# Turning the HGRN2 gate product on VectorE, with its moves pinned in the queue

## The chip, the cores and the metric

The program runs on 1 core of a Trainium2 chip. The metric is the device time of one execution in microseconds (us). Before the change the median of three runs is 398.56 us (398.11 to 400.23).

## The reference, cut to what matters

Two layers of a decoder trunk over 256 tokens of width 1024. In each layer one projection of the normalised input gives ten column groups of 512; three branches turn them into outputs, which are gated, joined and projected back:

```python
q_a, k_a, v_a, q_h, f_h, i_h, q_m, z = jnp.split(proj, split_points, axis=-1)
qa = partial_rope(rms_norm(q_a ..., moba_q_norm[l]), positions)
ka = partial_rope(rms_norm(k_a ..., moba_k_norm[l]), positions)
o_a = moba_attention(qa, ka, va).reshape(B, S, G)          # 8 heads of 64, causal
o_h = hgrn2_chunkwise(q_h, f_h, i_h, lb_all[l] ...)        # 4 heads of 128, gated recurrence
o_h = rms_norm(o_h, hgrn_o_norm[l]).astype(x.dtype).reshape(B, S, G)
o_m = memory_attention(qm, km, vm).reshape(B, S, G)        # 4 heads of 128, 256 memory tokens
y = jnp.concatenate([o_a, o_h, o_m], axis=-1) * jax.nn.silu(z)
x = x + y @ w_out[l]
```

All is f32. The part at issue is the middle third of `y`: `o_h` normalised per head, times its gain `hgrn_o_norm`, times `silu(z_h)`. The kernel calls it `zh`.

## The kernel before, in words

Every large product is made to f32 precision from two rounded parts: a weight tile of 128x1024 arrives by DMA as `wr`, ScalarE (ACT) casts it to the high part `wh` (L173, or L176 when a gain per row is multiplied in), VectorE (DVE) subtracts for the low part `wl` (L185 or L188), and TensorE (PE) runs three passes. `slot` keeps up to five loads, three `wh` and two `wl` ahead of PE. There are four `wr` buffers, three of `wh` and three of `wl`; a cast therefore waits until PE has read the tile three places earlier for the last time.

Each layer takes 60 such tiles in a fixed order: 8 of the memory's keys and values (first), forget logits, HGRN2 queries, MoBA keys, HGRN2 inputs, MoBA queries, `zh`, memory queries, MoBA values (4 tiles each), the gates of MoBA (A0 to A3 below) and of the memory branch (M0 to M3), and 12 tiles of `w_out`, those that multiply `zh` first (`KT_ORDER`).

The branches run as generators beside this stream: `step` moves each of them on by one `yield` at every half tile. That gives the program order, and so the priorities; the order in which each engine issues its instructions is then set by a scheduler that times the whole program by its own model. Instructions given to `keep_in_program_order` are not moved against each other; the weight loads go through `load`, which does that.

`zh` must stand with its columns on the partitions before `w_out` can use it. `y_transpose` (L733 to L747) does that: for each half of the tokens four PE transposes of 128x128 into a tile `sd` of PSUM (one of four side tiles), then ACT writes the high part with the gain (L740) and DVE the low part (L741). The keys of memory and MoBA and the MoBA probabilities `P` go another way, through `across` (L88 to L107): DVE turns blocks of 32x32 into `blk` (L94), a DMA writes `blk` to DRAM as `there` (L100), and four DMAs read it back with the blocks in place (L105). All of these are issued by the queue of SP, in between the weight loads. There is one `blk` buffer and there are two `there`.

The rotary tables `rtA` and `rtB` (L533 to L537) are made once by POOL, for both layers and for query and key; `g_qk` multiplies the projected keys or queries by them (`kr`, L896).

## Time and profile before

| | |
|---|---|
| median of the runs | 398.56 us (398.11 to 400.23) |
| the profiled execution, its own time | 399.08 us |
| its span | 397.3 us |
| PE, busy | 391.6 us (99%), 2887 matmuls |
| PE weight loads, busy | 326.9 us (82%) |
| DVE, busy | 312.2 us (79%) |
| ACT, busy | 258.4 us (65%) |
| POOL, busy | 53.0 us (13%) |
| DMA | 78.25 MB, mean 197 GB/s |

How to read it: times inside the trace count from the start of the span. PE's busy time covers matmuls that overlap in the array, so a pause shorter than a matmul's own length is not seen in it; the distance from one start to the next shows it. The granted clock of PE is full in every slice of the page. A row of the timeline gives the start, the length, engine, line, operation, tiles and count; for engines other than PE the start of the next row says how long an instruction held its engine, since neighbours overlap by about a tenth of a microsecond.

### The profile page before, as it was taken

What the parts mean: (1) busy time and instruction counts of PE and PEld (TensorE: products, weight loads), DVE (VectorE), ACT (ScalarE), POOL (GpSimd) and SP (SyncE); (2) the same over time, 40 slices, a digit from 0 to 9 for tenths busy, and PEclk for the clock granted to TensorE, in tenths of its full rate; (3) what the DMA queues carried; (4) which work ended last, traced back from release to release, by engine and by line L of the source; (5) the groups of instructions that cost most, each with busy time, mean ns of one, the idle gap of its engine ahead of it and who ended that gap; (6) DMA issues with size and microseconds to landing.
All of it is one profiled execution on the core that took longest, in us unless ns stands there. A gap on an engine that the chain in (4) does not pass through costs nothing.

```text
span 397.3 us, 7614 instructions
## 1 busy us (share of the span) xinstructions
PE 391.6 (99%) x2887; PEld 326.9 (82%) x2887; DVE 312.2 (79%) x604; ACT 258.4 (65%) x428; POOL 53.0 (13%) x79
## 2 busy tenths in 40 slices
PE   8999999999999999999999999999999999999996
PEld 6888888778788888878888888888888888888785
DVE  4789979898559997965577689899856799795643
ACT  5998756556768879554375776455855895982540
POOL 2013400704101200000000040031150030000000
PEclk9999999999999999999999999999999999999999
DMA  8976775368535997327554558544854188943522
GB/s 273 412 294 221 237 220 162 110 214 265 170 104 189 247 281 228 111 87 255 185 204 168 177 195 283 196 153 165 260 174 153 54 273 254 283 144 108 184 80 107
DMA packets 25509, 78.25 MB, mean 197 GB/s; under 512 B 3072, under 2 KB 7552, under 8 KB 25472
## 3 DMA queue, kind: packets, MB, share of 16 engines
q1 hardware_dynamic: 25184, 77.61, 59.3%
q8 instruction: 23, 0.38, 0.4%
q10 hardware_dynamic: 288, 0.15, 0.1%
q14 instruction: 14, 0.11, 0.1%
HBM read 71.46 MB, written 6.29 MB: 196 GB/s over the span
## 4 chain that ended last, share of the span: by engine, by line
PE 86%; DVE 6%; DMA 3%; POOL 2%; issue 1%; ACT 1%; SPq 0%; DVEq 0%; ACTq 0%
PE acc L227 58%; PE acc L1149 15%; PE sd L227 6%; PE sd L231 3%; DVE wl L185 2%; DMA kn<-there 1%; POOL rka L893 1%; PE sd L1112 1%; PE sd L440 1%; DMA gT<-in_gains_dram 1%; DMA there<-blk 1%; DVE blk L94 1%; ACT wh L173 1%; PE sd L737 0%; PE sd L1056 0%
## 5 line engine op out<-in xcount | busy, mean ns | idle before, releaser
L185 DVE TENSOR_TENSOR wl<-wr,wh 128x1024 fp32r<-128x1024 f32 x104 | 126.3, 1218 | 41.2 <-ACT wh L173 41.2
L173 ACT CAST wh<-wr 128x1024 fp32r<-128x1024 f32 x104 | 108.9, 1051 | 67.9 <-PE acc L227 37.2
L227 PE MATMUL acc<-wh,hT 128*128 128x512 f32 x384 | 124.8, 396 | 0.0
L227 PEld LDWEIGHTS acc<-wh,hT 128*128 128x128 f32 x384 | 71.8, 188 | 16.0 <-issue 0.7
L227 PE MATMUL acc<-wl,hT 128*128 128x512 f32 x192 | 75.2, 392 | 0.6 <-DVE wl L185 0.6
L227 PE MATMUL acc<-hT,wh 128*128 128x512 f32 x256 | 66.0, 395 | 0.0
L227 PEld LDWEIGHTS acc<-hT,wh 128*128 128x128 f32 x256 | 45.7, 189 | 8.6 <-ACT kn L595 0.4
L227 PEld LDWEIGHTS acc<-wl,hT 128*128 128x128 f32 x192 | 36.1, 188 | 7.8 <-DVE wl L185 0.9
L1149 PE MATMUL acc<-wl,yh 128*128 128x512 f32 (+1 forms) x96 | 37.4, 390 | 0.1
L227 PEld LDWEIGHTS acc<-hT,wl 128*128 128x128 f32 x256 | 35.1, 190 | 2.6
L1149 PE MATMUL acc<-wh,yl 128*128 128x512 f32 (+1 forms) x96 | 37.2, 388 | 0.0
L227 PE MATMUL acc<-hT,wl 128*128 128x256 f32 x256 | 36.4, 282 | 0.0
L1149 PE MATMUL acc<-wh,yh 128*128 128x512 f32 (+1 forms) x96 | 29.8, 388 | 0.0
L176 ACT ACTIVATE wh<-wr,gT 128x1024 fp32r<-128x1024 f32 (+1 forms) x21 | 19.4, 945 | 9.8 <-PE acc L227 4.0
L227 PE MATMUL acc<-wh,mTh 128*128 128x512 f32 x64 | 25.5, 401 | 0.2 <-DVE mTh L379 0.2
L188 DVE SCALAR_TENSOR_TENSOR wl<-wr,gT,wh 128x1024 fp32r<-128x1024 f32 (+1 forms) x21 | 21.0, 1027 | 5.7 <-ACT wh L176 5.7
L227 PE MATMUL acc<-wh,mTl 128*128 128x512 f32 x64 | 24.8, 390 | 0.0
L979 ACT ACTIVATE P<-P,nba,rq 128x128 f32<-128x128 f32 (+1 forms) x32 | 17.1, 537 | 8.1 <-DVE nba L973 8.1
L1149 PEld LDWEIGHTS acc<-wl,yh 128*128 128x128 f32 x96 | 18.0, 188 | 4.4 <-DVE wl L185 1.0
L1149 PEld LDWEIGHTS acc<-wh,yh 128*128 128x128 f32 x96 | 17.9, 188 | 3.9 <-ACT wh L173 0.4
L1149 PEld LDWEIGHTS acc<-wh,yl 128*128 128x128 f32 x96 | 18.0, 188 | 3.6
L227 PE MATMUL acc<-wl,mTh 128*128 128x512 f32 x64 | 20.2, 392 | 0.0
(220 smaller groups left out, 569.0 us busy)
## 6 DMA issues: line engine op xcount, KB each, us to landing
wr<-in_w_in_dram SPq DMA_DIRECT2D x80, 512.0 KB, 4.3
wr<-in_w_out_dram SPq DMA_DIRECT2D x24, 512.0 KB, 4.3
wr<-in_w_mem_kv_dram SPq DMA_DIRECT2D x15, 512.0 KB, 4.9
there<-blk SPq DMA_DIRECT2D x4, 768.0 KB, 3.7
PT<-there SPq DMA_DIRECT2D x16, 192.0 KB, 6.0
there<-blk SPq DMA_DIRECT2D x4, 512.0 KB, 3.2
xs<-in_x_dram SPq DMA_DIRECT2D x2, 512.0 KB, 8.4
memr<-in_mem_dram SPq DMA_DIRECT2D x2, 512.0 KB, 6.7
```

What stands on the lines that cost most here:

```text
L94: nc.vector.transpose(blk.rearrange("p c (n i) -> p c n i", n=n), src.rearrange("p (n c i) -> p c n i", n=n, c=4))
L173: nc.scalar.copy(whs[i], raws[i])
L176: nc.scalar.activation(whs[i][:, sl], raws[i][:, sl], AF.Copy, scale=gT[:, g:g + 1])
L185: nc.vector.tensor_tensor(wls[i], raws[i], whs[i].bitcast(F32), op=OP.subtract)
L188: ins = nc.vector.scalar_tensor_tensor(wls[i][:, sl], in0=raws[i][:, sl], scalar=gT[:, g:g + 1], in1=whs[i][:, sl].bitcast(F32), op0=OP.mu ...
L227: nc.tensor.matmul(o, lhsT=a, rhs=b, start=s, stop=e)
L231: tc.keep_in_program_order(nc.tensor.matmul(o, lhsT=a, rhs=b, start=True, stop=True))
L440: ins = nc.tensor.transpose(pt[:, j * 256 + t * 128:j * 256 + (t + 1) * 128], xn[t][:, k * 128:(k + 1) * 128], ident)
L893: nc.gpsimd.tensor_tensor(r[:, t8], ms[:, t8], pw[:, :8], op=OP.pow)
L979: nc.scalar.activation(P[:, i, kc[t]], P[:, i, kc[t]], AF.Exp, bias=nb[:, c:c + 1], scale=rq[:, r:r + 1], accum_out=sm[:, c:c + 1])
L1112: nc.tensor.transpose(pt[:, i * 256 + t * 128:i * 256 + (t + 1) * 128], P[:, t, i, b * 128:(b + 1) * 128], ident)
L1149: ins = nc.tensor.matmul(a, lhsT=y, rhs=wt[:, cs], start=n == (0 if to is None else nk - 2) and j == 0, stop=n == nk - 1 and j == 2)
```

## The change

Four things. `y_turned` takes the place of `y_transpose`: `zh` goes through `across` as the keys do, with the turned blocks staged in the buffer of the HGRN2 query (`hq0`, free by then), comes back into `zh` itself, and is split by `unstripped` (two casts on ACT, two subtractions on DVE). The gain `hgrn_o_norm` is multiplied into the four `w_out` tiles of that branch instead of into `zh`. The moves in `across` are issued with `load`, so the scheduler no longer moves them against each other or against the weight loads. The setup loses two of its `yield`s, makes the key's rotary tables before the query's, and gives control back only after layer 0.

```diff
-        nc.sync.dma_start(there.rearrange("q j c r -> (q j) c r"), blk)
+        load(there.rearrange("q j c r -> (q j) c r"), blk)
...
-            nc.sync.dma_start(dst[c * 32:c * 32 + 32], there[:, :, c].rearrange("q j r -> j q r"))
+            load(dst[c * 32:c * 32 + 32], there[:, :, c].rearrange("q j r -> j q r"))
...
+    def strip_of(o, t):
+        return o[:, :, t * 128:(t + 1) * 128].rearrange("p h (q i) -> p h q i", q=4)
+
+    def unstripped(oh, ol, a):
+        for t in range(2):
+            src, to = strips(a)[:, :, t], strip_of(oh, t)
+            nc.scalar.copy(to, src)
+            nc.vector.tensor_tensor(strip_of(ol, t), src, to.bitcast(F32), op=OP.subtract)
...
-            chunks.append(("O", dram(w_out, (l * DMIX + kt * 128) * D, [[D, 128], [1, D]]), None))
+            chunks.append(("O", dram(w_out, (l * DMIX + kt * 128) * D, [[D, 128], [1, D]]),
+                           GR_O + l if kt // 4 == H_ else None))
...
         periods(2, 0, 0.0)
         take(2, 0, 0, 1)
-        yield
         take(1, 11, 2, 3)
         take(2, 0, 2)
         take(0, 22, 3)
-        yield
...
-            for q in range(2):
+            for q in (1, 0):
...
-            yield
+                if l == 0:
+                    yield
...
-    def y_transpose(l, t, gain):
...
+    def y_turned(l):
+        flat = zh.rearrange("p t s -> p (t s)")
+        yield from turned(flat, "hq0")
+        unstripped(*y_tiles(H_), flat)
+        yield
+        for k in range(4):
+            done.add(f"y{4 * H_ + k}_{l}")
...
-        yield 2
-        for t in range(2):
-            yield from y_transpose(l, t, gT[:, GR_O + l:GR_O + l + 1])
+        yield from y_turned(l)
```

What it does to the order is seen on three engines. First ACT, layer 0, before: the casts of the gate tiles M1 (`wh_1865`), M2 (`wh_1903`) and M3 (`wh_1932`), and the exponentials of the two memory units (`P_1713` and `P_1781`).

```order
L173 CAST wh_1865<-wr_1773 128x1024
L310 COPY al_1910<-acc_1874 128x256
L712 ACT_TABLE_LOAD
L712 ACTIVATE sg_1888<-as_1825 128x512
L1094 ACT_TABLE_LOAD
L1094 ACTIVATE P_1713,smm0_1749<-sd_1714,nbm0_1748,qmr_1603 128x256 x2
L1094 ACTIVATE P_1713,smm0_1749<-sd_1715,nbm0_1748,qmr_1603 128x256 x2
L173 CAST wh_1903<-wr_1826 128x1024
L310 COPY al_1936<-acc_1913 128x256
L1094 ACTIVATE P_1781,smm1_1810<-sd_1782,nbm1_1809,qmr_1603 128x256 x2
L1094 ACTIVATE P_1781,smm1_1810<-sd_1783,nbm1_1809,qmr_1603 128x256 x2
L173 CAST wh_1932<-wr_1863 128x1024
```

The same place now; M1 is `wh_1857`, M2 `wh_1895`, the units are `P_1708` and `P_1769`.

```order
L183 CAST wh_1857<-wr_1761 128x1024
L320 COPY al_1902<-acc_1866 128x256
L721 ACT_TABLE_LOAD
L721 ACTIVATE sg_1880<-as_1815 128x512
L1092 ACT_TABLE_LOAD
L1092 ACTIVATE P_1708,smm0_1737<-sd_1709,nbm0_1736,qmr_1603 128x256 x2
L1092 ACTIVATE P_1708,smm0_1737<-sd_1710,nbm0_1736,qmr_1603 128x256 x2
L320 COPY al_1934<-acc_1905 128x256
L1092 ACTIVATE P_1769,smm1_1800<-sd_1770,nbm1_1799,qmr_1603 128x256 x2
L1092 ACTIVATE P_1769,smm1_1800<-sd_1771,nbm1_1799,qmr_1603 128x256 x2
L183 CAST wh_1895<-wr_1816 128x1024
L122 CAST yh1_1912<-zh_169 128x4x128 x2
```

The cast of M2 stood between the two units' exponentials and stands behind both now; the two casts of the turned `zh` follow it.

PE at the same place, before: the matmuls of M0 (`wh_1828`, `wl_1867`), of M1 (`wh_1865`, `wl_1905`) and the start of the first MoBA output product (`PT` by `va`, 8 matmuls in all, of which one row is shown).

```order
L227 MATMUL acc_1939<-hT_160,wh_1828 128x512 x8
L227 MATMUL acc_1939<-hT_160,wl_1867 128x256 x8
L227 MATMUL acc_1969<-hT_160,wh_1865 128x512 x6
L227 MATMUL sd_1976<-PT_1701,va_1796 64x256
```

PE now, from A2's second part (`wl_1765`) to the same product: A3 is `wh_1763`, M0 `wh_1818`, M1 `wh_1857`, M2 `wh_1895`.

```order
L237 MATMUL acc_1866<-hT_160,wl_1765 128x256 x8
L237 MATMUL acc_1905<-hT_160,wh_1763 128x512 x8
L237 MATMUL acc_1905<-hT_160,wl_1820 128x256 x8
L237 MATMUL acc_1937<-hT_160,wh_1818 128x512 x8
L237 MATMUL acc_1937<-hT_160,wl_1859 128x256 x8
L237 MATMUL acc_1967<-hT_160,wh_1857 128x512 x8
L237 MATMUL acc_1967<-hT_160,wl_1897 128x256 x8
L237 MATMUL acc_2033<-hT_160,wh_1895 128x512 x8
L237 MATMUL sd_1974<-PT_1696,va_1784 64x256
```

The MoBA product stood inside M1 and stands behind the first eight matmuls of M2 now; the memory scores that stood inside A3 (two groups of six) stand ahead of A2.

DVE in layer 0 where the keys meet their tables (`kr`), before:

```order
L766 TENSOR_TENSOR hQb_793<-hQ_712,hT4_1056 128x64x8
L767 TENSOR_TENSOR hK_565<-hKb_794,hT4_1056 128x64x8
L783 COPY_PREDICATED hSd_162<-mk_161,sd_970 128x256
L896 TENSOR_TENSOR kr_918<-acc_762,rtA_165 128x512
L896 TENSOR_TENSOR kr_918<-acc_763,rtA_165 128x512
```

And now:

```order
L767 TENSOR_TENSOR hQb_793<-hQ_712,hT4_1056 128x64x8
L895 TENSOR_TENSOR kr_918<-acc_762,rtA_165 128x512
L895 TENSOR_TENSOR kr_918<-acc_763,rtA_165 128x512
L768 TENSOR_TENSOR hK_591<-hKb_794,hT4_1056 128x64x8
L784 COPY_PREDICATED hSd_162<-mk_161,sd_970 128x256
```

The two products `kr` have moved ahead of the recurrence's `hK` and `hSd`.

The queue of SP at the end of layer 0's gates, now: `there_1694` is `zh`, `there_1748` and `there_1796` are the two halves of `P`; the `wr` are M1, M2, M3 and the first tile of `w_out`.

```order
L158 DMA there_1748<-blk_1697 128x1536
L158 DMA wr_1761<-in_w_in_dram 128x1024
L158 DMA zh_169<-there_1694 32x4x256 x2
L158 DMA there_1796<-blk_1751 128x1536
L158 DMA wr_1816<-in_w_in_dram 128x1024
L158 DMA zh_169<-there_1694 32x4x256 x2
L158 DMA PT_1696<-there_1748 32x4x384 x2
L158 DMA wr_1855<-in_w_in_dram 128x1024
L158 DMA PT_1696<-there_1748 32x4x384 x2
L158 DMA PT_1750<-there_1796 32x4x384 x2
L158 DMA wr_1893<-in_w_out_dram 128x1024
L158 DMA PT_1750<-there_1796 32x4x384 x2
```

Before, the first half of `P` was written three loads earlier and read back ahead of M0's load.

## Rows read from the trace of the kernel before

**Rows 1.** The page: busy time of PE, and the shares by engine of the chain that ended last.

```profile
PE 391.6 (99%) x2887; PEld 326.9 (82%) x2887; DVE 312.2 (79%) x604; ACT 258.4 (65%) x428; POOL 53.0 (13%) x79
...
PE 86%; DVE 6%; DMA 3%; POOL 2%; issue 1%; ACT 1%; SPq 0%; DVEq 0%; ACTq 0%
```

**Rows 2.** The timeline of PE, layer 0, at the first half of `zh`: start us, us, engine, line, operation, tiles, count.

```profile
133.22 0.60 PE L737 MATMUL sd<-ident,zh 128*128 128x128 f32 x4
133.57 0.37 PE L227 MATMUL sd<-kml,qmh 128*128 128x256 f32 x1
133.77 0.29 PE L227 MATMUL sd<-kmh,qml 128*128 128x256 f32 x1
```

**Rows 3.** The timeline of PE, layer 0, the gate tile A2 (its eight matmuls by `wh`, its eight by `wl`, and the next tile's start) and the first MoBA output product.

```profile
141.15 2.00 PE L227 MATMUL acc<-hT,wh 128*128 128x512 f32 x8
142.99 1.12 PE L227 MATMUL acc<-hT,wl 128*128 128x256 f32 x8
143.94 0.40 PE L227 MATMUL acc<-hT,wh 128*128 128x512 f32 x1
...
152.45 1.57 PE L227 MATMUL sd<-PT,va 128*64 128x256 f32 x16
```

**Rows 4.** The timeline of ACT, layer 0, from the cast of M1 to the cast of M3; in brackets the idle time before and what ended it. Left out are the sigmoid at 145.83 and the other exponentials.

```profile
143.19 1.06 ACT L173 CAST wh<-wr 128x1024 fp32r<-128x1024 f32 x1 [1.47 <-PE acc L227]
144.15 0.37 ACT L310 COPY al<-acc 128x256 f32<-128x256 f32 x1
144.53 1.28 ACT L712 ACT_TABLE_LOAD   x1
...
146.48 1.28 ACT L1094 ACT_TABLE_LOAD   x1
147.78 0.56 ACT L1094 ACTIVATE P<-sd,nbm,qmr 128x256 f32<-128x256 f32 x1
...
149.96 1.05 ACT L173 CAST wh<-wr 128x1024 fp32r<-128x1024 f32 x1
150.89 0.39 ACT L310 COPY al<-acc 128x256 f32<-128x256 f32 x1
151.16 0.59 ACT L1094 ACTIVATE P<-sd,nbm,qmr 128x256 f32<-128x256 f32 x1
...
153.34 1.07 ACT L173 CAST wh<-wr 128x1024 fp32r<-128x1024 f32 x1
```

**Rows 5.** DVE: the timeline of layer 0 behind the products `zh` (up to the turning of the second half of `P` and its end), and the turning of a tile of 128x1024 by the groups of the line L94 (duration ns min/median/max).

```profile
131.96 0.17 DVE L586 TENSOR_SCALAR qmm<-ssq 128x8 f32<-128x8 f32 x1
...
136.80 0.69 DVE L1087 TENSOR_REDUCE mxm<-sd 128x2 f32<-128x512 f32 x1
137.40 1.22 DVE L185 TENSOR_TENSOR wl<-wr,wh 128x1024 fp32r<-128x1024 f32 x1
138.54 1.77 DVE L94 STREAM_TRANSPOSE blk<-P 128x1536 f32<-128x1536 f32 x1
140.23 0.71 DVE L741 SCALAR_TENSOR_TENSOR yl<-sd,gT,yh 128x512 fp32r<-128x512 f32 x1
...
L94 DVE STREAM_TRANSPOSE blk<-kr x2: 1234/1234/1235, 83.9 to 272.2; 128x1024 f32<-128x1024 f32 x2
```

**Rows 6.** The timeline of PE, layer 0, in `w_out`, where the fourth tile begins.

```profile
175.53 1.14 PE L1149 MATMUL acc<-wh,yh 128*128 128x512 f32 x4
176.72 0.50 PE L1149 MATMUL acc<-wl,yh 128*128 128x512 f32 x1
177.06 0.39 PE L1149 MATMUL acc<-wh,yl 128*128 128x512 f32 x1
```

**Rows 7.** The timelines of POOL (two of the products of the rotary tables), of DVE and of PE, layer 0, where the keys meet their tables.

```profile
74.94 0.21 POOL L534 TENSOR_TENSOR rtA<-sc,mg 128x16 f32<-128x16 f32 x1
75.67 0.22 POOL L534 TENSOR_TENSOR rtA<-sc,mg 128x16 f32<-128x16 f32 x1
...
74.22 0.68 DVE L767 TENSOR_TENSOR hK<-hKb,hT 128x512 f32<-128x512 f32 x1
74.82 0.44 DVE L783 COPY_PREDICATED hSd<-mk,sd 128x256 f32<-128x256 uint8 x1
75.92 1.29 DVE L896 TENSOR_TENSOR kr<-acc,rtA 128x512 f32<-128x512 f32 x2 [0.66 <-POOL rtA L534]
77.65 1.21 DVE L185 TENSOR_TENSOR wl<-wr,wh 128x1024 fp32r<-128x1024 f32 x1
...
78.92 0.50 PE L227 MATMUL acc<-wl,hT 128*128 128x512 f32 x1 [0.58 <-DVE wl L185]
```

**Rows 8.** ACT's casts of whole weight tiles without and with a gain, by line and form: busy us, mean ns of one | idle before and its releasers.

```profile
L173 ACT CAST wh<-wr 128x1024 fp32r<-128x1024 f32 x104 | 108.9, 1051 | 67.9 <-PE acc L227 37.2 <-PE acc L1149 26.1 <-DMA wr<-in_w_in_dram 2.2
L176 ACT ACTIVATE wh<-wr,gT 128x1024 fp32r<-128x1024 f32 x11 | 12.6, 1152 | 6.1 <-PE acc L227 4.0 <-PE acc L1149 1.7 <-DMA wr<-in_w_mem_kv_dram 0.2
```

**Rows 9.** Three stretches of layer 0: length, busy us (and instructions) of PE, PEld, DVE, ACT and POOL, granted clock, busy share of the DMA engines, GB/s; and the reads of `PT` among the DMA issues (count, KB each, median us to landing).

```profile
129.00:139.00 10.00, 10.00 (x60) 8.70 (x58) 10.00 (x26) 8.10 (x17) 2.85 (x2) 1.00 0.97 247
139.00:149.00 10.00, 10.00 (x63) 8.99 (x62) 9.56 (x14) 7.76 (x13) 0.00 (x0) 1.00 0.91 282
149.00:159.00 10.00, 10.00 (x75) 8.17 (x74) 7.95 (x18) 9.82 (x23) 0.00 (x0) 1.00 0.72 225
...
PT<-there SPq DMA_DIRECT2D x16, 192.0 KB, 6.0
```

More of the change, by code (lines that the diff above doesn't have):

```diff
@@ L731, in y_store @@
             done.add(f"y{4 * br + k}_{l}")
-    def y_transpose(l, t, gain):
-        yield from room("sd")
-        pt = side_tile()
-        for j in range(4):
-            nc.tensor.transpose(pt[:, j * 128:(j + 1) * 128], zh[:, t, j * 128:(j + 1) * 128], ident)
-        p3 = heads(pt, 4)
-        oh, ol = (a[:, :, t * 128:(t + 1) * 128] for a in y_tiles(H_))
-        nc.scalar.activation(oh, p3, AF.Copy, scale=gain)
-        nc.vector.scalar_tensor_tensor(ol, in0=p3, scalar=gain, in1=oh.bitcast(F32), op0=OP.mult, op1=OP.subtract)
-        rel()
+    def y_turned(l):
+        flat = zh.rearrange("p t s -> p (t s)")
+        yield from turned(flat, "hq0")
+        unstripped(*y_tiles(H_), flat)
         yield
-        if t == 1:
-            for k in range(4):
-                done.add(f"y{4 * H_ + k}_{l}")
+        for k in range(4):
+            done.add(f"y{4 * H_ + k}_{l}")
     def g_hgrn(l):
@@ L1079, in g_mem_unit @@
                        (a, b) == passes[0], (a, b) == passes[2])
-        done.add(f"scores{u}{l}")
         yield
```

## The prediction

> **What bounds the kernel now.** I read the page's busy line and its chain first, then PE's timeline around each edit, then ACT and DVE at the same times, and the DMA share by stretch last. The page shows PE busy in 99% of the span and 86% of the chain on PE [rows 1]; the reader is to see that no other engine comes near it. So an instruction taken from PE is worth its length, and a cast that comes late for PE costs its lateness; work on ACT, DVE, POOL or a queue costs nothing until PE stands. The sum is made against the profiled execution, 399.08 us, which is 0.52 above the median of the runs, 398.56; the 0.52 comes off at the end. About 0.5%, or 2.0 us, is what a measurement of this kernel tells from no change: faster is below 396.6, slower above 400.5.
>
> **The transposes leave PE.** Four of them hold PE from 133.22 to the second matmul behind them at 133.77 [rows 2], 0.55 us, which contains one matmul of 256 columns. Eight of those take 0.95 us (142.99 to 143.94) [rows 3], so one is 0.12, and the four transposes are 0.43. Two halves in two layers are four such groups: **-1.72**. They stand in an unbroken row of matmuls, so nothing hides them.
>
> **The cast of M2 comes late.** Order on ACT decides this. M2's cast stood between the exponentials of the two memory units and now stands behind both. It also needs the buffer that A2's cast filled, as M1's cast did before it. I follow ACT from the moment PE has read A2's `wh` for the last time (142.99 in before) [rows 3, 4]: 0.20 until the cast of M1 begins, 0.96 for it, 0.38 for the copy `al`, 1.95 for the sigmoid with its table (144.53 to 146.48), 1.30 for the table of the exponentials, 2.18 for the first unit's four exponentials (147.78 to 149.96), 0.27 for the next `al`, 2.18 for the second unit's (151.16 to 153.34), and 1.07 for M2's cast. That is 10.49 us. PE meanwhile has A2's low part, 0.95, and the tiles A3, M0 and M1. A tile is 1.84 + 0.95 = 2.79 [rows 3], so PE comes to M2 after 0.95 + 8.37 = 9.32. The MoBA product (1.57) [rows 3] that stood inside M1 and would have covered the difference stands behind M2's first eight now, and the memory's score groups that stood inside A3 stand ahead of A2. PE waits 10.49 - 9.32 = 1.17 in each layer: **+2.34**. Everything on PE is queued behind that matmul.
>
> The bounds of this term: it is 0 if ACT gains 1.17 somewhere in the chain (a shorter wait ahead of the sigmoid, an exponential that overlaps more). It is 1.57 more per layer at most, if the second unit's scores were late by as much as the product that moved; I take the sum of the rows, since each link is a start-to-start distance that was measured in this place.
>
> DVE could lengthen the same chain, since the sigmoid reads what DVE writes. From 131.96 to 140.23 DVE has 8.27 us of work that stays [rows 5]. Into it come the turning of `zh` (1.23 for a tile of that size), one more `mxm` (0.60), one `wl` (1.14) and an addition `as` (I put it at 0.3, an estimate of a quarter of the `wl`), so the second half of `P` is turned at about 143.5, and behind two more `mxm`, a `wl` and an `as` the sigmoid's input is there at about 146.2. ACT comes to the sigmoid at about 142.99 + 0.56 + 0.20 + 0.96 + 0.38 = 145.1 plus the table's 1.28 [rows 4], 146.4, where 0.56 is the shift of A2: twelve score matmuls at 0.119 ahead of it, less 0.86 for the transposes gone. So DVE is hidden with 0.2 to spare; what it is later than that adds to the 1.17.
>
> Behind M2's cast stand the two casts of the turned `zh`, then a copy, a table, a sigmoid and M3's cast. With half a tile cast at 0.52 (from 1051 ns for a whole one) [rows 8] and the others as above, M3 is ready just when PE has done M2 and the product. I cost it at nothing; if that cover is gone it is some tenths more.
>
> **w_out.** The fourth tile shows a pause: from 175.53 to 177.06 are 1.53 us for five matmuls [rows 6], which at 1.84 / 8 = 0.23 are 1.15. The 0.38 is the wait for `wl`, whose cast waits for the first tile's last matmul. In the new order twelve memory matmuls and nine others (about 3.5 us) stand between that last matmul and the need, against 2.6 us of cast and subtraction, so the pause goes: **-0.76** in two layers. What is late next is nothing that I find there. The gain in these four tiles makes their cast 1152 instead of 1051 ns [rows 8], 0.10 each, hidden in that same slack; without it, 0.8 in all.
>
> **The rotary tables.** The key's second product now ends where the first row of [rows 7] ends, 75.15, not 75.89. But `kr` has moved ahead of `hK` and `hSd`. DVE is done with what stands ahead of it at 74.22 and waits 0.96 to about 75.18, then does the same work. Before, it did `hK` and `hSd` in that time and waited 75.92 - 75.16 = 0.76 at most. The `wl` behind it at 77.65, for which PE waits at 78.92 [rows 7], comes 0.20 later: **+0.20**. If only the tables had moved, `kr` would have started 0.7 earlier and PE's pause there (0.58) would have gone.
>
> **The moves.** `zh` adds a write and a read of 0.52 MB each per layer in stretches in which the DMA engines are busy 0.97, 0.91 and 0.72 of the time, at 247, 282 and 225 GB/s [rows 9]. The queue holds the order now: the write of `P`'s second half waits for DVE (143.5), and all reads of `PT` stand behind it. I put its start at 144.4, an estimate. Then 2.88 MB are queued up to the last read of the first `PT` (0.79 for the write, a tile M2 and half of `zh` with 0.79, half of `PT` 0.39, M3 0.52, the other half 0.39) and 4.19 MB up to the last of the second. PE wants the first at 142.99 + 0.56 + 10.49 + 1.84, about 155.9, and the second after a product, M2's low part and M3's first eight, about 160.3. At 282 GB/s they land at 154.6 and 159.3, in time; at 247 the second lands at 161.4, 1.1 late; at 225 the first is 1.25 late and the second 1.5 more. The value taken is 0, since 139 to 149 is the row most like it; the ends are 0 and 2.7 per layer.
>
> The Trainium skill ("VectorE: DVE Perf Modes", The three transpose paths and Rules for kernel authors) says that DVE transposes only within 32x32 blocks and that a 128x128 transpose is better left to TensorE. The rows agree in this: the turning of `P` is followed by four reads of 192 KB that take 6.0 us to land. By that page the change would lose, by the mechanism of the second rival below.
>
> **The sum.** -1.72 - 0.76 + 2.34 + 0.20 = +0.06, so 399.14 for the profiled execution and **398.6** against the median.
>
> **Rivals.** *M2's cast isn't late.* Then -1.72 - 0.76 + 0.20 = -2.28, 396.3. For it: 1.17 is a difference of two sums of ten, and if PE is later by any pause of its own between A2 and M2, the wait shrinks by that. Against it: every link is in the rows, and ACT has no idle time left there in which to gain. It decides once some 1.0 of the 1.17 is gone in each layer; less leaves the time within no change.
>
> *The transfers are late (the slower side).* One place: the reads of `PT` behind the write that waits for DVE. If the engines move less than 4.19 MB / (160.3 - 144.4) = 264 GB/s, the second half of the MoBA product stalls PE. At 247 it costs 2 x 1.1 = 2.2, so 400.8; at 225, 2 x 2.7, so 404. For it: 247 and 225 are what the rows beside show, and the blocks are written and read in small pieces. Against it: at 0.72 the engines weren't full, so 225 was demand and not their limit; 282 / 0.91 is 310.
>
> *The reorder of the recurrence doesn't cost.* The part on the tables would then do something other than the order says. If DVE takes `kr` without a longer wait, the +0.20 becomes up to -0.66 and the time is 397.7, which can't be told from no change.
>
> The chances: the forecast 0.46 (with its own range 396.5 to 400.6, so 0.04 of it below and 0.05 above the bounds of no change), the first rival 0.28, the second 0.21, the third 0.05. Faster is 0.28 + 0.04 = 0.32, slower 0.21 + 0.05 = 0.26, no change 0.42. The range from 395.8 to 401.8 takes in the first rival with half a microsecond below it and the second as far as 247 GB/s with one above.
>
> **What would show it.** The PE group of `y_transpose` is gone and PE has 16 matmuls fewer. Ahead of M2's first matmul, near 154 and as far into layer 1, PE pauses 1.1 to 1.2, ended by ACT's cast; no pause there, and the first rival holds. The fourth tile of `w_out` starts its low part without 0.38. `kr` starts near 75.2 with 0.96 idle ahead of it. The reads of `PT` land before PE's product begins; if PE's product waits for `PT` or a tile's load behind them, it is the second rival. I am wrong if a pause of over half a microsecond appears at a place not named here, M3's cast or the recurrence behind the moved `kr` first.

## The result and the profile after

The changed kernel takes 403.28 us (four runs, 401.87 to 404.66), the kernel before 398.34 beside it: a ratio of 1.0102, 95% interval 1.0072 to 1.0132. It is slower, and outside the range that was forecast. The four runs are two near 401.9 and two near 404.65; the profile is of the first kind (401.92, span 400.1), and what the two near 404.65 have more is in no trace here. So the account below is of the 2.8 us between the two spans, 397.3 and 400.1. That is one profile of each kernel: the second profile of the changed kernel, below, is 1.6 us longer and has 1.7 us more of the same waits.

The page of the changed kernel: busy time and the chain, against [rows 1].

```profile
PE 388.9 (97%) x2871; PEld 325.1 (81%) x2871; DVE 315.2 (79%) x606; ACT 258.9 (65%) x428; POOL 51.8 (13%) x79
...
PE 71%; DMA 12%; DVE 10%; issue 2%; POOL 1%; SPq 1%; ACT 1%; DVEq 0%; ACTq 0%
```

PE has lost its 16 transposes and 2.7 us of busy time, and DMA has gone from 3% of the chain to 12%. PE's timeline shows where, layer 0 from M1's second part to the second MoBA product, then the same three places of layer 1.

```profile
151.34 1.11 PE L237 MATMUL acc<-hT,wl 128*128 128x256 f32 x8
153.98 2.11 PE L237 MATMUL acc<-hT,wh 128*128 128x512 f32 x8 [1.53 <-ACT wh L183]
156.02 1.57 PE L237 MATMUL sd<-PT,va 128*64 128x256 f32 x16
157.52 1.23 PE L237 MATMUL acc<-hT,wl 128*128 128x256 f32 x8
158.59 2.00 PE L237 MATMUL acc<-hT,wh 128*128 128x512 f32 x8
161.15 1.54 PE L237 MATMUL sd<-PT,va 128*64 128x256 f32 x16 [0.55 <-DMA PT<-there]
...
347.82 2.11 PE L237 MATMUL acc<-hT,wh 128*128 128x512 f32 x8 [1.04 <-ACT wh L183]
350.80 1.54 PE L237 MATMUL sd<-PT,va 128*64 128x256 f32 x16 [0.86 <-DMA PT<-there]
...
356.56 1.54 PE L237 MATMUL sd<-PT,va 128*64 128x256 f32 x16 [1.23 <-DMA PT<-there]
```

From start to start, against the pace of [rows 3]: M2's cast is 1.69 late (153.98 less 151.34 + 0.95) and 1.20 in layer 1. `PT` is late by 0.7 (161.15 less 158.59 + 1.84), 1.0 and 1.4. That is **2.9 us for the cast and 3.1 for the moves**. The chain of waits, the same stretch of layer 0, tells what stands behind the moves:

```profile
134.35 7.35 DMA there<-blk
141.69 0.03 issue
...
141.79 1.79 DVE blk L94
...
143.59 0.34 SPq L158
...
146.45 6.07 DMA PT<-there
152.52 0.02 issue
152.53 8.47 DMA PT<-there
161.01 0.14 issue
161.15 1.54 PE sd L237 x16
```

It is to be read from below: PE waits for the last read of the second `PT`. That waits for its place behind the other reads, these for the write of `P`'s second half, its turning for the one `blk` buffer, and that for the write of `P`'s first half, which went out at 134.35. DVE had turned that half between 123.51 and 125.29:

```profile
123.51 1.78 DVE L94 STREAM_TRANSPOSE blk<-P 128x1536 f32<-128x1536 f32 x1
...
131.63 1.20 DVE L94 STREAM_TRANSPOSE blk<-zh 128x1024 f32<-128x1024 f32 x1
```

and the queue of SP held it for 9 us, behind the write of `zh` and a load:

```profile
132.86 0.33 SPq L158 DMA_DIRECT2D there<-blk  x1
133.97 0.33 SPq L158 DMA_DIRECT2D wr<-in_w_in_dram  x1
134.35 0.45 SPq L158 DMA_DIRECT2D there<-blk  x1
```

In the kernel before, the same write went out 0.03 us after the turning. This last link is a small one, though. DVE stood only 0.48 us for it:

```profile
141.79 1.78 DVE L94 STREAM_TRANSPOSE blk<-P 128x1536 f32<-128x1536 f32 x1 [0.48 <-DMA there<-blk]
```

The second half is turned by 143.57 here and by 140.31 in before. Most of those 3.3 us are thus the order, which has the turning of `zh` and other work of DVE ahead of it. The prediction had reckoned with that (143.5). In the three stretches of [rows 9] the changed kernel has:

```profile
129.00:139.00 10.00, 10.00 (x58) 8.77 (x58) 10.00 (x25) 7.12 (x14) 2.26 (x2) 1.00 0.76 256
139.00:149.00 10.00, 10.00 (x62) 8.91 (x61) 8.94 (x14) 6.61 (x10) 0.00 (x0) 1.00 0.73 238
149.00:159.00 10.00, 8.47 (x56) 6.92 (x55) 7.18 (x17) 9.36 (x23) 0.00 (x0) 1.00 1.09 262
```

The engines are full in the last one (1.09, up from 0.72) and move no more than 262 GB/s. A share over 1.00 means that packets overlap on an engine, so a packet's time is not its own alone. The packets of the trace say what fills the stretch. Those of a weight tile, 4096 bytes, take 159 ns (median; mean 191), which by the median is 412 GB/s on 16 engines. Those of the reads of `PT`, 1536 bytes, take 122 ns (mean 116), which is 201 GB/s. Added up, the two `PT` of a layer, 1.57 MB, are 7.4 us of all engines. In packets of a weight tile as many bytes would be 3.8 us by the median, 4.6 by the mean.

### The profile page after: what moved, and what is told of

Same layout as the page of the kernel before. It is cut to its first block, busy times and chain, and to the rows that moved or that the text cites. A ratio compares the mean times of both kernels' runs of the same rounds, so it can differ in the third digit from the quotient of the medians.

```text
span 400.1 us, 7594 instructions
## 1 busy us (share of the span) xinstructions
PE 388.9 (97%) x2871; PEld 325.1 (81%) x2871; DVE 315.2 (79%) x606; ACT 258.9 (65%) x428; POOL 51.8 (13%) x79
## 4 chain that ended last, share of the span: by engine, by line
PE 71%; DMA 12%; DVE 10%; issue 2%; POOL 1%; SPq 1%; ACT 1%; DVEq 0%; ACTq 0%
PE acc L237 46%; PE acc L1147 16%; DMA PT<-there 8%; PE sd L237 5%; PE sd L241 3%; DMA there<-blk 3%; DVE wl L195 2%; DMA kn<-there 1%; DVE blk L94 1%; POOL rka L892 1%; SPq L158 1%; PE sd L1110 1%; DMA gT<-in_gains_dram 1%; PE sd L450 1%; DVE zh L875 1%
## 5 line engine op out<-in xcount | busy, mean ns | idle before, releaser
L195 DVE TENSOR_TENSOR wl<-wr,wh 128x1024 fp32r<-128x1024 f32 x96 | 117.1, 1221 | 39.5 <-ACT wh L183 39.5
L183 ACT CAST wh<-wr 128x1024 fp32r<-128x1024 f32 x96 | 100.5, 1051 | 62.5 <-PE acc L237 40.3
L237 PE MATMUL acc<-hT,wh 128*128 128x512 f32 x256 | 65.0, 393 | 2.6 <-ACT wh L183 2.6
L198 DVE SCALAR_TENSOR_TENSOR wl<-wr,gT,wh 128x1024 fp32r<-128x1024 f32 (+1 forms) x29 | 31.2, 1098 | 9.2 <-ACT wh L186 9.0
L186 ACT ACTIVATE wh<-wr,gT 128x1024 fp32r<-128x1024 f32 (+1 forms) x29 | 28.6, 1003 | 14.9 <-DMA wr<-in_w_out_dram 5.2
```

The lines of the kernel that those rows point to most:

```text
L183: nc.scalar.copy(whs[i], raws[i])
L186: nc.scalar.activation(whs[i][:, sl], raws[i][:, sl], AF.Copy, scale=gT[:, g:g + 1])
L195: nc.vector.tensor_tensor(wls[i], raws[i], whs[i].bitcast(F32), op=OP.subtract)
L198: ins = nc.vector.scalar_tensor_tensor(wls[i][:, sl], in0=raws[i][:, sl], scalar=gT[:, g:g + 1], in1=whs[i][:, sl].bitcast(F32), op0=OP.mu ...
L237: nc.tensor.matmul(o, lhsT=a, rhs=b, start=s, stop=e)
```

## The experiments

Two things were in dispute: whether the late moves come from the pinned order or from the bytes of `zh`, and what the late cast is worth. `Theory` and `rival` stand in each expectation. The kernel before ran beside each group on the same chip, at 398.7 to 400.6.

**The tables alone.** The kernel before with the part of the change in `setup`.

```diff
-            for q in range(2):
+            for q in (1, 0):
...
-            yield
+                if l == 0:
+                    yield
```

> The kernel before with the part on the rotary tables alone (two yields gone, the key's tables first). Only DVE's order changes, at one place: the products kr ahead of hK and hSd. Theory: POOL's first table product took 0.76 us in the kernel before because DVE's hK ran beside it, and takes 0.21 now that kr has moved ahead of hK; so kr starts earlier, near 74.6 instead of 75.92, PE's pause of 0.86 at 77.83 shrinks to about 0.3, and the time falls by 0.55 to about 398.0. Rival, as the prediction had it: DVE waits 0.96 for the second product and everything behind is 0.20 later, about 398.7.

Measured: 0.999 (0.9967 to 1.0014), so by time alone it can't be told from no change; the profile tells. POOL's first products and DVE around them, against [rows 7]:

```profile
73.64 0.22 POOL L531 TENSOR_TENSOR rtA<-sc,mg 128x16 f32<-128x16 f32 x1
73.82 0.22 POOL L532 TENSOR_TENSOR rtA<-sc,mg 128x16 f32<-128x16 f32 x1
...
75.44 0.67 POOL L534 TENSOR_TENSOR rtB<-rt,mg 128x16 f32<-128x16 f32 x1
...
74.07 1.29 DVE L895 TENSOR_TENSOR kr<-acc,rtA 128x512 f32<-128x512 f32 x2 [0.36 <-POOL rtA L532]
75.28 0.75 DVE L766 TENSOR_TENSOR hK<-hKb,hT 128x512 f32<-128x512 f32 x1
```

The first product of the tables took 0.76 us in before, when DVE's `hK` began at the same 74.22. Here it takes 0.22, and the product that is slow, 0.67, is the one that runs beside `hK` now. `kr` starts 1.85 earlier (`hQb` ahead of it 0.58), and PE's wait of 0.58 for the `wl` behind it is gone. The theory holds. The Trainium skill ("SBUF — State Buffer", SBUF: two separate sides) says that a DVE instruction with two SBUF inputs and a GpSimd one lock the same ports for a whole instruction; the two slow products agree with that. This run's profile has 1.3 us of another kind at 255, the recurrence of layer 1, where the key moves landed at 249.7 instead of 247.6. No edit is there, and the transfers go out in the same order. A weight tile issued among them took 6.5 us to land instead of 4.0, and what slowed them wasn't found. The same place costs 1.9 us in the profiles of pe_turn and m2_first and 1.8 in that of no_zh_moves, below, so a part of those times need not be the edit's.

**Not pinned.** The changed kernel, the moves as in before.

```diff
-        load(there.rearrange("q j c r -> (q j) c r"), blk)
+        nc.sync.dma_start(there.rearrange("q j c r -> (q j) c r"), blk)
```

> The changed kernel with the moves issued as before, not pinned among the loads. The four reads of the first PT stand ahead of the write of P's second half again, and M2's cast stands between the exponentials; zh makes its way as in the changed kernel, with the same bytes. Theory (it is the pinned order): no wait of PE for PT or for M2's cast, -1.7 for the transposes, -0.55 for the tables, up to -0.8 in w_out: 395.5 to 396.5. Rival (it is the bytes of zh): the reads of PT land a microsecond or more late in each layer all the same, 398.5 or more.

Measured: 1.013 (1.0094 to 1.0167). `PT` is late by 2.4 in layer 0 and 2.8 in layer 1. Here, too, the write of `P`'s first half stood behind that of `zh` and went out 8 us after its turning. The theory as put, that it is the pin, falls; the rival is not proved, since the queue held the write all the same. In layer 0 PE also waits 0.7 us for M2's cast, which the theory had excluded.

**zh on PE again.** The changed kernel with `y_transpose` and the gain as before; pins and tables stay.

```diff
-        yield from y_turned(l)
+        for t in range(2):
+            yield from y_transpose(l, t, gT[:, GR_O + l:GR_O + l + 1])
```

> The changed kernel with zh turned on PE as before (transposes, gain on zh, no move of zh), the moves pinned and the tables as changed. M2's cast stands between the exponentials, so no wait there. Theory (it is the pinned order): the reads of the first PT stand behind the write of P's second half, 2.6 MB from about 141 on, and at 230 to 280 GB/s land near 150.5 to 152.5, while PE wants them in the middle of M1, at about 148 to 149: 2 to 3 us of wait in each layer, 402 to 404. Rival (it is the bytes of zh, which are gone here): PT in time, and only the tables' -0.55 is left, 398.0.

Measured: 1.0111 (1.0068 to 1.0154); waits for `PT` of 1.1 and 3.1 us, and the write of `P`'s first half 7.9 us after its turning, behind a load. So the order of the changed kernel, with its pins, is enough to be late without a byte of `zh`. The first product came in time, unlike expected.

**M2's cast first.** The changed kernel with the cast of M2 pinned ahead of the second unit's exponentials.

```diff
+                if i in (46, 106):
+                    tc.keep_in_program_order(ins)
...
+        while u and st["h"] < 47 + 60 * l:
+            yield
```

> The changed kernel with M2's cast held ahead of the second unit's exponentials (both in program order); the queue of SP has the same order, the product of the first PT stands behind M2's second part instead of its first. Theory (the reads of PT set when PE goes on): the waits for M2's cast, 1.69 and 1.20, go, but the last reads of the second PT land at the same times (161.0 and 356.5), so PE waits there by as much longer and the time stays within 0.6 of the changed kernel's 401.9. Rival (the waits add up): 2.9 less, 399.0.

Measured: 1.0157 (1.0115 to 1.02), span 405.2. M2's wait is gone and `PT` has taken its place, in layer 0:

```profile
157.24 1.54 PE L239 MATMUL sd<-PT,va 128*64 128x256 f32 x16 [1.45 <-DMA PT<-there]
159.11 2.11 PE L239 MATMUL acc<-hT,wh 128*128 128x512 f32 x8 [0.32 <-ACT wh L183]
162.43 0.83 PE L239 MATMUL sd<-PT,va 128*64 128x256 f32 x7 [1.22 <-DMA PT<-there]
```

The waits don't add up: as long as `PT` is late, the cast costs nothing more (over both layers 6.5 us of waits for `PT`, where the changed kernel has 6.0 for `PT` and the cast). It is even slower than the changed kernel, with 1.9 us in the recurrence of layer 1, as in the run on the tables, and the clock (below).

**A queue of its own.** Not pinned, and the moves of `zh` issued by POOL's queue; then the same with M2's cast first.

```diff
+        dma = nc.gpsimd if stage else nc.sync
...
+        dma.dma_start(there.rearrange("q j c r -> (q j) c r"), blk)
```

> The changed kernel with the moves not pinned and those of zh issued on POOL's queue instead of SP's: the same bytes, the same turning on DVE, the same tables. In SP's queue P's first half is written where it was before the change, ahead of three loads; in no_pin and in the changed kernel that write stood behind zh's write and went out 8 to 9 us after P was turned. Theory (the write of P's first half stands behind other moves and loads in one queue, and all reads of PT follow from it): the write goes out within half a microsecond of the turning, no wait of PE for PT over 0.3 us, and the time is 2.3 to 3.0 us under the kernel before, a ratio of 0.992 to 0.994. Rival (the bytes of zh fill the DMA engines): PT lands late all the same, a microsecond or more of wait in each layer, ratio over 0.997.

> As zh_own_queue, and M2's cast held ahead of the second half of the second unit's exponentials. In this order both MoBA products stand ahead of M2 on PE (3.1 us more cover). If so, M2's cast was hidden already and this changes nothing: within 0.3 us of zh_own_queue. If the cast of M2 still ends late there, this is 1 us or more faster than zh_own_queue.

Measured: 1.0264 (1.0229 to 1.0299) and 1.009 (1.0056 to 1.0124). The write of `P`'s first half still went out 4 us after the turning, behind a load, and then took 7.0 us to land. The reads of the second `PT` landed at 159.2, and the scheduler, which reckoned with less, had put their product ahead of M2: PE waits 3.9 in each layer. The two runs differ by far more than the 0.3 expected. That product has another place in each: PE waits 3.9 and 3.9 us for `PT` in the first, 2.2 and 1.5 in the second. The clock granted to PE differs too, by the mean 0.986 against 0.996. The theory falls here; what the second run was for, M2's cast, it doesn't tell.

**The changed kernel again.**

> The changed kernel once more beside the others, for the comparison on one chip: 1.008 to 1.015 of the kernel before by its four runs so far; waits of PE for M2's cast and for PT as in its first profile, 2.9 and 3.1 us, and the write of P's first half 9 us behind its turning.

Measured: 1.0122 (1.0084 to 1.0161); 2.1 and 1.2 for the cast, 0.3, 0.9, 1.6 and 1.5 for `PT`. As expected, with the waits for `PT` 1.2 longer in sum.

**The bytes alone, and the order alone.** The kernel before with a write of `zh` and four reads that nobody uses, from POOL's queue; and the changed kernel without those moves (the middle third of `y` is then not turned in place), once more with M2's cast held.

```diff
+        nc.gpsimd.dma_start(out_there.rearrange("q j c r -> (q j) c r"), flat.rearrange("p (c r) -> p c r", c=4))
+        for c in range(4):
+            nc.gpsimd.dma_start(spare[c * 32:c * 32 + 32], out_there[:, :, c].rearrange("q j r -> j q r"))
```

> The kernel before, and in each layer one more write of zh to DRAM (0.52 MB) and four reads of it in pieces of 1024 bytes into the free hq0 buffer, issued on POOL's queue at the time at which the changed kernel moves zh; nothing reads them. The order on PE, DVE, ACT and SP is that of before, instruction by instruction. In before the last read of the second PT landed at 152.5 and PE wanted it at about 155.3, 2.8 us of slack. The packets of zh are about 3 us of all 16 DMA engines in each layer. Theory A (the bytes alone use up the slack and no more): 0 to 0.7 us of wait in each layer, ratio 1.000 to 1.004. Theory B (the bytes alone explain the change's loss): 1.5 us or more in each layer, ratio over 1.007. Theory C (bytes don't matter): the loads and PT land as in before, ratio 1.000 and PT's last read within 0.5 us of before's.

Measured: 1.0115 (1.0073 to 1.0157). ACT, DVE and SP keep the order of before here, and PE's changes only by neighbours that trade places, so this is the cleanest of the runs, and it is theory B: the bytes alone are enough to make `PT` late. The last read of the second `PT` landed at 158.5, 5.9 us later than in before, though the packets of `zh` add up to 3.6 us of the engines: it is also behind transfers that were themselves pushed into this stretch. PE waits 2.7 and 1.8, in sum 4.5, where the changed kernel waits 3.1 (4.4 in its second profile). That the whole time comes out like the changed kernel's is a coincidence: that one has 3.0 us of gains and 2.9 for the cast besides, and this one has a stretch of lower clock (below). The stretches of [rows 9] in this kernel:

```profile
129.00:139.00 10.00, 10.00 (x57) 8.62 (x56) 10.00 (x25) 8.57 (x18) 2.71 (x3) 1.00 0.95 249
139.00:149.00 10.00, 10.00 (x65) 9.09 (x64) 10.00 (x15) 7.34 (x11) 2.28 (x4) 1.00 0.96 316
149.00:159.00 10.00, 7.45 (x49) 5.89 (x50) 7.54 (x19) 9.76 (x23) 0.00 (x0) 0.95 1.06 246
```

> The changed kernel with zh turned by DVE but without its moves to DRAM and back: the casts read zh as it stood, so that third of y has its columns in the wrong place. All else is as changed, pinned moves and tables too. The scheduler puts the first MoBA product ahead of M2 here, which gives M2's cast 1.6 us more cover. If the pinned order were enough for the loss (theory order): PT lands a microsecond or more late in each layer, ratio over 0.998. If bytes and order are both needed (theory both): the reads of PT land 2 to 4 us earlier than in the changed kernel, at 152.5 and 157.5 as in pe_turn, in time for PE in this order; the time then has the gains alone, -1.7 for the transposes, -0.5 for the tables, up to -0.8 in w_out: ratio 0.992 to 0.995.

> As no_zh_moves, and M2's cast held ahead of the second half of the second unit's exponentials; PE has the first eight of M2 ahead of the first MoBA product again. With the transfers in time (theory both) a wait for M2's cast of 0 to 0.5 us in each layer is left and the time is within 0.8 us of no_zh_moves. With PT late (theory order) the product waits 1.8 us later and the time is as in no_zh_moves too, but above 0.998 of before. If M2's cast is the larger part of the loss, both of these runs are 2 us or more under the kernel before.

Measured: 1.0196 (1.0144 to 1.0247) and 1.008 (1.004 to 1.012). In the first PE waits 3.2 and 3.3 us for the first `PT`, whose last read landed at 158.1: theory order. The scheduler had moved its product ahead of M2, so PE wanted it earlier than in the changed kernel. In the second run M2's cast was as late as before (152.88), because the copies and exponentials ahead of it had moved too; it says nothing on the cast. It does say something on the order: PE has the changed kernel's order there, and without a byte of `zh` it waits 0.8, 0.5 and 2.1 us for `PT`. So bytes alone are enough (4.5 us of waits for `PT`) and order alone is enough (3.4), and together they cost no more than either (3.1 and 4.4 in the two profiles). Each kernel wants `PT` at a time of its own, so these sizes can't be compared more finely.

**Wide reads.** If the strided reads are what fills the engines, the blocks can be put in place on the way out. The same bytes, in pieces of 1536 on the write, and one read over all 128 partitions.

```diff
+        for q in range(4):
+            load(there[:, :, q].rearrange("c j r -> j c r"), blk[q * 32:q * 32 + 32])
...
+        load(dst, there.rearrange("c j q r -> (c j) q r"))
```

> The changed kernel with the blocks put in place on the way out instead of on the way back: four writes of 32 partitions each, in pieces of 1536 bytes (P) or 1024 (zh), then one read over 128 partitions in pieces of 6144 or 4096 bytes. Same bytes, moves still pinned; in the queue M2's cast still stands behind both units' exponentials, the second MoBA product moves behind M3's second part. In the changed kernel's trace the 1536-byte packets of the reads took 122 ns each (median) against 84 ns for 2048 bytes and 234 ns for 6144, so the two PT of a layer cost 7.7 us of all 16 engines instead of 3.8. Theory (the small pieces of the reads are slow, as reads into 32 partitions or out of DRAM): the waits for PT, 3.1 us in both layers together, fall under 1.0, the wait for M2's cast stays near 1.2 in each layer: ratio 1.000 to 1.005. Rival (pieces of 1536 bytes are as slow as writes, or the bytes and the place in the queue decide): PT as late as before, ratio 1.008 to 1.015.

> The same wide reads, moves not pinned. In this order the write of P's second half follows P's first read, and PE has the first MoBA product around M2's first matmuls, the second inside M3. Theory: with the reads of PT at full rate they land in time (waits for PT under 0.5 us in each layer), M2's cast is covered by the product ahead of it, and the gains show: -1.7, -0.5 and up to -0.8, ratio 0.992 to 0.996. Rival (the bytes in this stretch are too many however they are cut): a wait of 1 us or more in each layer for PT, ratio over 1.000.

Measured: 1.0046 (1.0027 to 1.0065) and 1.0043 (1.0027 to 1.006). With the pins and the order of the changed kernel, the waits for `PT` fall from 3.1 to 0.65 us and its last read lands at 159.3. Against the last of the three stretches above:

```profile
149.00:159.00 10.00, 8.43 (x56) 6.81 (x56) 7.33 (x17) 9.97 (x24) 0.00 (x0) 1.00 1.00 390
```

390 GB/s where the changed kernel had 262, with the engines busy 1.00 of the time. From the write of the second half to the last read, the same 4.19 MB and the loads issued among them, it is 322 GB/s against 263. The gain is in the reads: both `PT` of a layer are 3.8 us of all engines as rows of 6144 bytes, where they were 7.4. The pieces of 1536 bytes are no quicker for being written: in this stretch the second half's write took 119 ns for each (median; mean 107). The theory holds for the pinned kernel. What is left is M2's cast, 1.5 and 1.2 us. The profile is of the fastest of this kernel's executions, 399.48 where their median is 400.43, so about 1 us of the time is not explained by it. In the second run `PT` is in time, but M2's cast is not covered: 1.2 and 0.7 us, with 0.25 more for M3's in each layer. Whether the gains that were expected come can't be read from the time of this run: PE is 1.65 us behind the kernel before by its 61st matmul (17.17 against 15.52), in a stretch that no edit touches.

**Wide reads and M2's cast first.** Both with the edit of m2_first; and the wide reads in the kernel before, with the tables and without the rest of the change.

> wide_reads with M2's cast held ahead of the second unit's exponentials, as in m2_first. Theory (two separate costs, the late moves and the late cast, of which the first hid the second in m2_first): with PT nearly in time the cast's 2.7 us now count. M2's wait goes; PE comes to the first product about 0.6 us earlier than in wide_reads, so its wait grows to 0.8 to 1.2 us in each layer. Net 1.2 to 2.2 us under wide_reads: ratio 0.998 to 1.002 of before. Rival (as in m2_first, PT takes up all of it): ratio 1.003 to 1.007, the time of wide_reads.

> wide_reads_no_pin with M2's cast held ahead of the second half of the second unit's exponentials. There PE waited 1.21 and 0.71 us for that cast and for nothing else in these stretches. Theory: the cast ends 1.1 us earlier, both waits shrink to 0.1 or go, 1.7 us less: ratio 0.999 to 1.001, and if the gains of the change are all there, under 1. Rival (the next thing, PT's second read or M3's cast, takes its place): within 0.5 us of wide_reads_no_pin, ratio 1.003 to 1.005.

> The kernel before with the tables' part and the wide reads, zh on PE and nothing pinned. In before PE waits for no PT (2.8 us of slack), so wide reads alone should bring nothing there: the tables' 0.5 us, ratio 0.997 to 1.001. If it is under 0.996, the reads cost the kernel before something that its profile did not show as a wait.

Measured: 1.0029 (1.001 to 1.0048), 1.0037 (1.0013 to 1.0061) and 0.9973 (0.9956 to 0.9989). PE in wide_m2, layer 0:

```profile
153.28 2.14 PE L237 MATMUL acc<-hT,wh 128*128 128x512 f32 x8 [0.54 <-ACT wh L181]
155.25 1.10 PE L237 MATMUL acc<-hT,wl 128*128 128x256 f32 x8
156.66 1.57 PE L237 MATMUL sd<-PT,va 128*64 128x256 f32 x16 [0.31 <-DMA PT<-there]
159.66 2.10 PE L237 MATMUL acc<-hT,wh 128*128 128x512 f32 x8 [1.43 <-ACT wh L181]
```

The wait goes from M2's cast to M3's: 0.7 for M2, 0.5 for `PT` and 1.6 for M3, where wide_reads had 1.5 for M2 and 0.4 for `PT`. M2's cast had nothing of ACT ahead of it any more; it stood for its load, which landed at 152.16:

```profile
152.18 1.05 ACT L181 CAST wh<-wr 128x1024 fp32r<-128x1024 f32 x1 [1.37 <-DMA wr<-in_w_in_dram]
```

So ACT was idle just ahead of it, and the exponentials, a table and a sigmoid came behind that cast and ahead of M3's, which began at 158.58. What is left of the wait is in good part a transfer again. In wide_no_pin_m2 PE waits 1.1 for M2 and 1.4 for M3; there M2's cast did not wait for its load, but went between two pairs of exponentials, at 157.43. Neither theory priced that: both had only M2 in view, and M3's "just ready" of the prediction was the point. The third run is the one that is faster than both kernels. It has the tables' part, and no wait for `PT` either way; its interval overlaps that of the tables alone, so nothing shows that the wide reads add anything by themselves.

## Why the prediction was wrong, by its steps

- **What bounds it.** Right. The difference is waits of PE and matmuls fewer, to within 0.2 us (the sum below).
- **The transposes, -1.72.** Right: 16 matmuls fewer, and an unbroken row of matmuls in their place.
- **The cast of M2, +2.34.** Right in mechanism, place and nearly in size: 1.20 in layer 1 against 1.17. In layer 0 it is 1.69, and the 0.49 more are the load of M1, which landed at 143.55, when PE had freed the buffer at 142.96. That is a rival's mechanism reaching into this term. The rows of ACT (the first names the turning of `P` as the releaser, which ended at the same time as the load; in the second run of this kernel the profile names the load):

```profile
143.65 1.05 ACT L183 CAST wh<-wr 128x1024 fp32r<-128x1024 f32 x1 [1.96 <-DVE blk L94]
...
148.23 0.56 ACT L1092 ACTIVATE P<-sd,nbm,qmr 128x256 f32<-128x256 f32 x1
...
152.85 1.07 ACT L183 CAST wh<-wr 128x1024 fp32r<-128x1024 f32 x1
```

From the start of M1's cast to that of M2's are 9.2 us, as the sum had it (10.49 less 0.20 and 1.07).
- **w_out, -0.76.** Right. At the fourth tile, four matmuls take the 0.93 that they should, against [rows 6]:

```profile
176.46 1.09 PE L1147 MATMUL acc<-wh,yh 128*128 128x512 f32 x4
177.39 0.39 PE L1147 MATMUL acc<-wl,yh 128*128 128x512 f32 x1
```

- **The rotary tables, +0.20.** Wrong in sign: about -0.5. The failed step is "The key's second product now ends where the first row of [rows 7] ends, 75.15". It took the 0.76 of POOL's first product for its own length; that was its length beside `hK`, and `hK` is what the change moved away. The order had it, and the row had it; the two weren't read together.
- **The moves, 0.** This is the step that decided: "the value taken is 0, since 139 to 149 is the row most like it". The count of bytes was right. So was the time at which PE would want the second `PT` (160.3; it was 160.4), but that is in part luck: PE was through with A2's `wh` 0.6 us sooner than reckoned, and M1's load, which came too late by as much, made up for it. The rate was not right: from 143.59 to 161.01 the 4.19 MB went at 241 GB/s, not 282, and in layer 1, from 337.38 to 356.47, at 220. The prediction's own bounds, 247 and 225, were the right ones, and 264 was given as the point from which it decides. The rate was taken from a stretch with other things in it. The row of 139 to 149 in before holds 0.59 MB of reads of `PT` in its 2.82 MB, with the engines at 0.91. The stretch in question holds all eight reads (1.57 MB, 7.4 us of all engines) and 0.38 MB of loads issued meanwhile, which the count left out, and its packets add up to 17.6 us of the 16 engines in 17.4 us: they were full. The pieces alone don't account for that. By the mean packet times of before the 4.19 MB would be 15.1 us, and 16.2 with those loads; the packets themselves took longer here, those of the weight tiles 210 ns by the mean instead of 191. Why they did is open.
- **The second rival** is what happened, with its mechanism; it had a chance of 0.21 and a price of 2.2 to 5.4, of which 3.1 came in the profiled execution. The write of `P`'s first half, held for 9 us, was not in it, but that added only the 0.48 us for which DVE stood.
- The sum with the measured terms: -1.7 - 0.8 - 0.5 + 2.9 + 3.1 = +3.0, against 2.8 between the spans.
- The rule that was weighed there, of the Trainium skill ("VectorE: DVE Perf Modes", Rules for kernel authors), that a 128x128 transpose is better left to TensorE, was on the right side in this kernel: no run that turns `zh` on DVE was faster than before. The price here is not the turning but the moves behind it.

## What to carry to other kernels

The GB/s of a neighbouring stretch is not the rate at which a queue empties when it is full. Count what stands in it: the small pieces by their own packets' duration, which here was half the rate of whole tiles, and the loads that are issued meanwhile. Even that comes out some 1 us short here, so take a margin. Before a transfer is added, count the slack of the last one that PE needs (2.9 us in before, layer 0) against everything that is in flight around it, and look at which write is queued behind which load when a move is pinned among loads that are issued tiles ahead. And where a wait is to be taken from one instruction, look at what that instruction and the next ones wait for: here M2's cast, put first, stood 1.37 us for its load, and the wait went on to M3's.

## What the runs showed of the hardware

A piece of 1536 bytes took 122 ns (median; 115 in before) in the strided reads from DRAM into 32 partitions, longer than the 84 ns of a 2048-byte piece. As a piece of a write from 32 partitions it took 65 ns in wide_reads (mean 86), but 119 in wide_before (mean 107), so the direction does not decide it. The reads of `zh` have the same form, in pieces of 1024 bytes, and took 46 ns in the same stretch (mean 58). The Trainium skill ("DMA: Bandwidth & Descriptors", Why small descriptors are slow (HBM only)) lays the cost of small pieces to a fixed part per packet; that can't make a smaller packet slower than a larger one, so here the measurement decides. The cause (the stride, the 32 partitions, the size, or what runs beside) was not separated.

A wait of PE costs more than its length once it is long. The clock granted to PE, and the rows behind the wait, in pe_turn (a wait of 3.1 us that ends at 357.07):

```profile
350.00:354.00 4.00, 4.00 (x29) 2.93 (x27) 3.39 (x8) 3.60 (x7) 0.00 (x0) 1.00 1.07 243
354.00:358.00 4.00, 1.04 (x7) 0.65 (x8) 1.99 (x4) 1.58 (x2) 0.00 (x0) 0.80 0.95 344
358.00:362.00 4.00, 4.00 (x29) 3.28 (x26) 2.99 (x6) 3.01 (x5) 0.00 (x0) 0.77 0.46 155
...
357.07 2.85 PE L236 MATMUL sd<-PT,va 128*64 128x256 f32 x16 [2.96 <-DMA PT<-there]
```

The product takes 2.85 us instead of 1.54. It is the same in bytes_only behind a wait of 2.7 us (clock 0.75 from 156 to 160 and 0.82 from 160 to 164). In zh_own_queue_m2 the clock fell behind a wait of 2.2 us (0.61 from 156 to 160), and in pe_turn also behind two waits of 0.9 and 1.0 within 2.3 us (0.65 from 258 to 262). In the changed kernel's two profiles, with waits up to 1.7 and 2.1, it stays at 1.00 there. The Trainium skill ("TensorE: Matmul & The Clock Gate", Part 1) puts the halving at an idle window of about 3.4 us; the runs here show it behind shorter waits, from 2.2.
